# An attention loop on transposed scores, with maxima from a half-depth pass and float32 value products

## The chip, the cores and the metric

The kernel runs on one core of a Trainium2 chip, as one launch. The metric is the device time of that launch in microseconds. Five engines work side by side and wait for one another through semaphores: PE multiplies matrices, DVE and ACT do vector and scalar work and read PE's results out of PSUM, POOL does element-wise work on SBUF, and SP issues the DMAs here.

## The reference

The reference is a two-layer encoder trunk on 1024 tokens of width 1024, all in float32. Only the attention of the first layer is touched:

```python
def attend_block(q_blk):
    scores = jnp.einsum('bkgqd,bksd->bkgqs', q_blk, kt).astype(jnp.float32)
    p = jax.nn.softmax(scores, axis=-1).astype(vt.dtype)
    return jnp.einsum('bkgqs,bksd->bkgqd', p, vt)
...
return o @ w_o
```

There are 16 query heads and 4 key/value heads of 64 dimensions; q and k are normalised and rotated before. After the attention come the output projection, a cross-attention into 256 memory tokens and a gated MLP; the second layer has a pooling mixer in place of the attention.

## The kernel before

PE multiplies in a fast reduced form of float32 (`F32R`). To keep the precision, every operand x is split into a high part (rounded) and a low part (x minus high). `mm3` (lines 756 to 758) makes a product of three: high by high, high by low, low by high. Its helpers are `self.high` on ACT (line 669) and `self.low` on DVE (line 672). Most of the kernel's PE time is `mm3`.

The operands lie in slots: 20 tiles `R` of 128 x 2048, handed out whole or by halves by `Slots`. `self.scr()` gives scratch tiles of 128 x 1024, `self.psA()` PSUM tiles of two banks and `self.psB()` of one bank.

Stages are mostly ordered by `Plan`. A stage adds operations with a kind (which gives engine and assumed time), what they read, write and take; `Plan.run` then simulates the engines and writes the instructions of each engine in the order that comes out. On the chip the engines keep that order, whatever their real times are. The order within PE is the order in which the products were added.

The QKV stage (a `Plan`) makes q, k and v. For each token block k is split and transposed into `K[0]` and `K[1]`: 64 rows high on 64 rows low, and low on high. q is transposed into `Q[kv, half]` with high rows above low rows. So the two products `K[0]` and `K[1]` with q add up all four parts. v is kept as high and low columns in `V`. At the end of the stage three score units are computed ahead of the loop (`plan_scores`).

The attention loop is an order written out by hand (lines 1174 to 1296). A unit is 128 queries of one head. There are 128 units: four pairs of query blocks, 16 heads, two blocks. For each unit:

- `score` (line 789): four products of 512 columns put 128 queries x 1024 keys into a PSUM tile pA.
- `peak` (line 1189): DVE reduces to the negative maximum; `softmax`: ACT takes exp with the sum (line 1195), POOL the inverse (line 1197) and the scaling (line 1198).
- `turn` (line 1209): eight transposes on PE; ACT copies the high parts (line 1211) and DVE makes the low parts (line 1216) into `PT`.
- `values` (lines 1231, 1232), once for two units: 16 products of 256 columns, keys on the rows, high and low columns of v as weights; ACT and DVE add both halves (lines 1237, 1243), POOL splits the result into `OT` (lines 1246, 1247).

The loop is skewed: while PE computes the scores of a unit, the transposes and values are those of units two and three before it. Behind the loop `run` loads the output weights (`load_rows`) and starts the output products, two token blocks of each half first.

Of the kernel before, what the change touches and what calls it, by code (L numbers as in the profile page):

```python
# [16 lines left out]
P = 128  # L17
# [25 lines left out]
       *((h, g, t) for h in range(2) for g in range(4) if h or g > 1 for t in range(4 * h, 4 * h + 4)),  # L43
       ("V", 4), ("S", 0), ("V", 5), ("S", 1), ("V", 6), ("S", 2), ("V", 7))
LAG = 4
WARM = 20, 8
# [116 lines left out]
class Plan:  # L163
# [8 lines left out]
             "tiny": ("DVE", 0.1, 0.0, 0.1), "scale": ("POOL", 0.0, 0.45, 0.12), "load": ("SP", 0.0, 1.6, 2.3)}  # L172
# [458 lines left out]
class Kernel:  # L631
# [140 lines left out]
    def attention(self):  # L772
# [5 lines left out]
        units = [(j, hh, i) for j in range(NT // 2) for hh in range(NH) for i in range(2)]  # L778
        Q, prs, OT, sums = {}, {}, [], {}

        def score(u):
            j, hh, i = units[u]
            kv = hh // 4
            c0 = (j % 2 + 2 * i) * P
            q = R.v(Q[kv, j // 2], 4)[:, hh % 4, c0:c0 + P]
            s = self.psA()
            for kh in range(2):
                for part in range(2):
                    nc.tensor.matmul(s[:, kh * 512:(kh + 1) * 512], q,  # L789
                                     R.v(K[part][kh], 4)[:, kv],  # L790
                                     start=part == 0, stop=part == 1)
            return s

        with tc.tile_pool(name="qk", bufs=1, reuse_waits="tile") as qk, self.psum("psq", 1, 6) as self.ps:
# [222 lines left out]
            def plan_k(t, b):  # L1017
# [7 lines left out]
                def high():  # L1025
                    at[half] = R.get_half()
                    nc.scalar.activation(view(at[half])[:, :, 0:3:2], q3()[:, :, None, :].to_broadcast([P, 4, 2, HD]), AF.Copy)

                def low():
                    kst = view(at[half])  # L1030
                    nc.vector.tensor_tensor(out=kst[:, :, 1], in0=q3(), in1=kst[:, :, 0].bitcast(F32), op=OP.subtract)
# [5 lines left out]
            def plan_turn_k(t):  # L1037
                half = ("kst", t)
                for i in range(2):
                    b = ("kturned", t, i)  # L1040

                    def turn(i=i, b=b):
                        kst = R.hv(at[half])[:, :768].rearrange("p (h i c) -> p h i c", h=4, i=3)
                        p = at[b] = self.psB().rearrange("p (a b) -> p a b", a=4)
                        for h in range(4):
                            nc.tensor.transpose(p[:, h, :], kst[:, h, i:i + 2].rearrange("p a b -> p (a b)").bitcast(F32),
                                                self.ident)

                    def put(i=i, b=b):
                        o = R.v(K[i][t // 4], 4)[:, :, (t % 4) * P:(t % 4 + 1) * P]  # L1050
                        (nc.vector.tensor_copy if i else nc.scalar.copy)(o, at.pop(b))
# [3 lines left out]
            def plan_q(it, b):  # L1055
# [3 lines left out]

                def high():  # L1060
                    at[st] = qk.tile([P, 4, 2 * HD], F32R, name="qst", bufs=3)
                    self.high(at[st][:, :, :HD], q3())

                def low():
                    self.low(at[st][:, :, :HD], at[st][:, :, HD:], q3())
# [21 lines left out]
            def plan_scores(u):  # L1087
                j, hh, i = units[u]
                s, kv = ("s", u), hh // 4
                x = ("pr", u)  # L1090

                def emit():
                    at[s] = score(u)

                def biggest():
                    at["nm", u] = self.stat(1, "nm")
                    nc.vector.tensor_reduce(at["nm", u], at[s], axis=AX.X, op=OP.max, negate=True)

                def exp():
                    prs[u], at["sum", u] = self.scr(), self.stat(1, "sum")  # L1100
                    nc.scalar.activation(prs[u], at[s], AF.Exp, bias=at["nm", u], accum_out=at["sum", u])

                def inverse():
                    at["inv", u] = self.stat(1, "inv")
                    nc.vector.reciprocal(at["inv", u], at["sum", u])

                def scale():
                    nc.gpsimd.tensor_scalar(prs[u], prs[u], at["inv", u], 1.0, op0=OP.mult, op1=OP.mult)
                plan.add("product", 4, emit, [("KT", t, i) for t in range(NT) for i in range(2)] +
                         [("QT", kv, j // 2, t) for t in range(j // 2 * 4, j // 2 * 4 + 4)], [s], [("A", s)])  # L1110
                plan.add("tap", 1024, biggest, [s], [("nm", u)], uses=[s])
                plan.add("square", 1024, exp, [s, ("nm", u)], [x], [("scr", None)], [s], late=4.0)
                plan.add("tiny", 1, inverse, [x], [("inv", u)], late=6.0)
                plan.add("scale", 2.7, scale, [("inv", u), x], [x], late=7.0)

            def main():
# [7 lines left out]
                for it in QKV:  # L1124
                    kind, t = it[0], it[-1]
                    if kind == "S":
                        plan_scores(t)
# [44 lines left out]
            R.put(*sets[1])  # L1172

        self.ps = self.ctx.enter_context(self.psum("ps", 2, 4))
        with tc.tile_pool(name="at", bufs=1, reuse_waits="tile") as at:
            PT = [[at.tile([P, 2048], F32R, name=f"PT{i}{j}") for j in range(2)] for i in range(2)]
            def parts(u):
                return (x.rearrange("p (a b) -> p a b", a=8) for x in PT[u // 2 % 2])

            S, nm, T = {}, {}, {}  # L1180

            def scores(u):
                if u not in prs:
                    S[u] = score(u)

            def peak(u):
                if u in S:
                    nm[u] = self.stat(1, "nm")
                    nc.vector.tensor_reduce(nm[u], S[u], axis=AX.X, op=OP.max, negate=True)  # L1189

            def softmax(u):
                if u in S:
                    pr = prs[u] = self.scr()
                    rs = self.stat(1, "sum")
                    nc.scalar.activation(pr, S.pop(u), AF.Exp, bias=nm.pop(u), accum_out=rs)  # L1195
                    ri = self.stat(1, "inv")
                    nc.gpsimd.tensor_tensor(out=ri, in0=rs, in1=self.minus, op=OP.pow)
                    nc.gpsimd.tensor_scalar(pr, pr, ri, 1.0, op0=OP.mult, op1=OP.mult)  # L1198

            def pieces(u, g):  # L1200
                c = slice(u % 2 * P, (u % 2 + 1) * P)
                return (x[:, 4 * g:4 * g + 4, c] for x in parts(u))

            def turn(u, g):
                if u in prs:
                    p = T[u, g] = self.psB().rearrange("p (a b) -> p a b", a=4)
                    for k in range(4):
                        b = 4 * g + k
                        nc.tensor.transpose(p[:, k, :], prs[u][:, b * P:(b + 1) * P], self.ident)  # L1209
                    hi, _ = pieces(u, g)  # L1210
                    nc.scalar.copy(hi, p)  # L1211

            def low(u, g):
                if (u, g) in T:
                    hi, lo = pieces(u, g)
# [1060 lines left out]
```

## Time and profile before

| | us |
|---|---|
| median of 3 runs | 2498.35 (2497.17 to 2500.2) |
| span of the profiled execution | 2493.0 |
| median less that span | 5.35 |
| PE busy | 2474.6 |
| DVE busy | 1991.6 |
| ACT busy | 1351.0 |
| POOL busy | 462.1 |

The times of single instructions come from the profiled execution. The durations of matmuls overlap, since PE is a pipeline: the distance between the starts of two of them says what one costs. In rows on an instruction line, three durations with slashes are minimum, median and maximum in ns, followed by the first and the last start in us. In rows of groups the numbers behind the bar are busy us and mean ns, then idle time before them. In rows in order of time the first number is the start, the second the duration. A row of a stretch gives its length and then the busy time of PE, of the weight loads (PEld), DVE, ACT and POOL, the granted clock of PE (1.00 is full), and the DMA share.

### The profile page before, as it was taken

How to read it: one execution, taken by the hardware profiler on the slowest of the kernel's cores; microseconds unless marked ns; L12 is line 12 of the kernel's file. 1: busy time of each engine (PE TensorE's matmuls, PEld its weight loads, DVE VectorE, ACT ScalarE, POOL GpSimd, SP SyncE). 2: the span in 40 equal slices, each digit the busy share in tenths (PEclk: the TensorE clock that was granted, in tenths of full speed). 3: DMA queues.
4: the chain of work that ended last, by engine and by line, in shares of the span. 5: the costliest groups of instructions: out<-in, count | busy, mean ns of one | idle time of the engine just before them, and what ended most of it. 6: DMA issues, size and time to landing. Idle time of an engine off the chain costs nothing.

```text
span 2493.0 us, 37178 instructions
## 1 busy us (share of the span) xinstructions
PE 2474.6 (99%) x13510; PEld 2138.3 (86%) x13510; DVE 1991.6 (80%) x2839; ACT 1351.0 (54%) x2326; POOL 462.1 (19%) x658
## 2 busy tenths in 40 slices
PE   9999999999999999999999999999999999999998
PEld 9999999988899888888888888889888888888887
DVE  7879999974986389888889676997469888888875
ACT  6558888862655255455555334655345545554542
POOL 5767777731011000000000003102010000000001
PEclk9999999999999999999999999999999999999999
DMA  5300000042585124343258553388123324337852
GB/s 170 100 4 1 2 1 1 2 165 69 202 311 181 62 70 127 89 123 106 85 178 290 196 176 112 128 299 300 65 72 114 110 85 127 106 93 257 276 193 98
DMA packets 310124, 320.73 MB, mean 129 GB/s; under 512 B 13229, under 2 KB 244765, under 8 KB 309941
## 3 DMA queue, kind: packets, MB, share of 16 engines
q1 hardware_dynamic: 309941, 318.35, 38.8%
q8 instruction: 107, 1.75, 0.3%
q14 instruction: 76, 0.62, 0.1%
HBM read 230.91 MB, written 82.58 MB: 126 GB/s over the span
## 4 chain that ended last, share of the span: by engine, by line
PE 93%; issue 2%; DVE 2%; POOL 1%; ACT 1%; DMA 1%; SPq 0%; POOLq 0%; ACTq 0%; DVEq 0%
PE pB L756 22%; PE pB L758 22%; PE pB L757 22%; PE pA L789 5%; PE pB L1209 4%; PE pA L758 3%; PE pA L756 3%; PE pA L757 3%; PE pB L1231 2%; PE pB L1232 2%; PE pB L325 1%; DVE R L672 1%; PE pB L1072 1%; PE pA L2164 0%; DMA scr<-X 0%
## 5 line engine op out<-in xcount | busy, mean ns | idle before, releaser
L756 PE MATMUL pB<-R,R 128*128 128x512 f32 (+1 forms) x2732 | 1014.8, 371 | 1.8 <-ACT R L669 0.9
L758 PE MATMUL pB<-R,R 128*128 128x512 f32 (+1 forms) x2728 | 1007.6, 369 | 1.7 <-DVE R L672 1.6
L757 PE MATMUL pB<-R,R 128*128 128x512 f32 (+1 forms) x2732 | 1008.8, 369 | 0.2 <-DVE R L672 0.2
L756 PEld LDWEIGHTS pB<-R,R 128*128 128x128 f32 x2732 | 514.7, 188 | 90.9 <-ACT R L669 2.1
L758 PEld LDWEIGHTS pB<-R,R 128*128 128x128 f32 x2728 | 513.9, 188 | 89.5 <-DVE R L672 3.5
L757 PEld LDWEIGHTS pB<-R,R 128*128 128x128 f32 x2732 | 514.9, 188 | 87.1 <-DVE R L672 1.2
L669 ACT ACTIVATE R<-scr 128x512 fp32r<-128x512 f32 (+2 forms) x340 | 256.8, 782 | 214.9 <-DMA scr<-Gs 59.8
L729 POOL TENSOR_SCALAR ms<-ss 128x1 f32<-128x1 f32 (+2 forms) x97 | 32.1, 331 | 1651.7 <-ACT R L737 1279.9
L672 DVE TENSOR_TENSOR R<-X,R 128x512 fp32r<-128x512 f32 x374 | 252.0, 685 | 67.8 <-ACT R L669 67.1
L669 ACT ACTIVATE R<-X 128x512 fp32r<-128x512 f32 x374 | 231.8, 630 | 132.9 <-PE pB L757 64.0
L672 DVE TENSOR_TENSOR R<-scr,R 128x512 fp32r<-128x512 f32 (+2 forms) x328 | 275.0, 867 | 26.6 <-ACT R L669 26.2
L439 ACT COPY scr<-pB 128x512 f32<-128x512 f32 x156 | 91.3, 585 | 180.6 <-PE pB L758 173.3
L1852 DVE TENSOR_TENSOR X<-pB,X 128x512 f32<-128x512 f32 (+1 forms) x145 | 99.2, 685 | 80.4 <-PE pB L758 79.6
L1216 DVE TENSOR_TENSOR PT<-pB,PT 128x512 fp32r<-128x512 f32 x256 | 159.1, 683 | 4.2 <-ACT PT L1211 2.9
L1189 DVE TENSOR_REDUCE nm<-pA 128x1 f32<-128x1024 f32 x125 | 152.2, 1218 | 4.3
L756 PE MATMUL pA<-R,R 128*128 128x512 f32 (+1 forms) x420 | 150.6, 359 | 0.0
L758 PE MATMUL pA<-R,R 128*128 128x512 f32 (+1 forms) x420 | 150.2, 358 | 0.0
L757 PE MATMUL pA<-R,R 128*128 128x512 f32 (+1 forms) x420 | 149.9, 357 | 0.0
L1195 ACT ACTIVATE scr<-pA,nm 128x1024 f32<-128x1024 f32 x125 | 142.4, 1139 | 5.6 <-DVE nm L1189 3.5
L789 PE MATMUL pA<-R,R 128*128 128x512 f32 x512 | 144.7, 404 | 0.3 <-ACT scr L1195 0.3
L1198 POOL TENSOR_SCALAR scr<-scr,inv 128x1024 f32<-128x1024 f32 x125 | 141.2, 1129 | 12.3
L1211 ACT CAST PT<-pB 128x512 fp32r<-128x512 f32 x256 | 131.0, 600 | 1.2 <-PE pB L1209 1.2
(184 smaller groups left out, 3582.5 us busy)
## 6 DMA issues: line engine op xcount, KB each, us to landing
X<-in_ffn_w_up SPq DMA_DIRECT2D x82, 512.0 KB
Gs<-X SPq DMA_DIRECT2D x105, 256.0 KB
scr<-in_ffn_w_down SPq DMA_DIRECT2D x45, 512.0 KB
scr<-Gs SPq DMA_DIRECT2D x35, 512.0 KB
scr<-in_xattn_w_kv SPq DMA_DIRECT2D x32, 512.0 KB
scr<-Gs SPq DMA_DIRECT2D x42, 384.0 KB
scr<-in_attn_w_qkv SPq DMA_DIRECT2D x22, 512.0 KB
Wt<-scr SPq DMA_DIRECT2D x44, 256.0 KB
```

Of the source, the lines that this page charges most:

```text
L669: self.nc.scalar.activation(hi, src, AF.Copy)
L672: self.nc.vector.tensor_tensor(out=lo, in0=src, in1=hi.bitcast(F32), op=OP.subtract)
L756: mm(out, ah, bh, start=start, stop=False)
L757: mm(out, ah, bl, start=False, stop=False)
L758: mm(out, al, bh, start=False, stop=stop)
L789: nc.tensor.matmul(s[:, kh * 512:(kh + 1) * 512], q, R.v(K[part][kh], 4)[:, kv], start=part == 0, stop=part == 1)
L1189: nc.vector.tensor_reduce(nm[u], S[u], axis=AX.X, op=OP.max, negate=True)
L1195: nc.scalar.activation(pr, S.pop(u), AF.Exp, bias=nm.pop(u), accum_out=rs)
L1198: nc.gpsimd.tensor_scalar(pr, pr, ri, 1.0, op0=OP.mult, op1=OP.mult)
L1209: nc.tensor.transpose(p[:, k, :], prs[u][:, b * P:(b + 1) * P], self.ident)
L1211: nc.scalar.copy(hi, p)
L1216: nc.vector.tensor_tensor(out=lo, in0=T.pop((u, g)), in1=hi.bitcast(F32), op=OP.subtract)
```

## The change

The loop is rebuilt as a `Plan` on scores that have keys on the rows and queries on the columns, so that no transposes are needed behind the softmax. A group is 512 queries (`half`) and two heads; there are 16 groups, 8 of each half.

- **K and Q.** `K[0]` now holds the high part twice, on both row halves. `K[1]` holds the low part on 64 rows and, written by POOL (`plan_ones`), a row of ones below. In `Q` the high rows stand above for one head of a pair and below for the other.
- **Maxima.** `peaks` (line 789 in the new file) computes high by high only, for the two heads at once: one on rows 0 to 63, the other on rows 64 to 127, each a product of 64 rows and 512 columns into its own bank. DVE reduces (`biggest`), the two key halves are joined (`joined`), and `shift` brings them as a row to slot half `qm` by eight DMAs of 128 elements, next to two DMAs that copy the high rows of q there. Those of group 0 are made in the QKV stage, where the three score units stood, those of later groups five steps ahead.
- **Scores.** `plan_scores` makes 128 keys x 512 queries with two products: `K[0]` with Q, and 65 rows of `K[1]` with `qm`. The row of ones adds the negative maximum, so ACT takes exp without a bias and writes float32 to `pt`.
- **Values.** v's two parts are added once into `V32` (POOL). `plan_values` multiplies in full float32, `V32` as weights of 64 columns; the two heads go to the two column halves (output rows 0 to 63 and 64 to 127). DVE and POOL add up the exps of the eight key blocks (`acc`), and `plan_sum` sums them over the keys with a float32 product against ones.
- **Scaling.** The sums go by DMA to 8 x 128, DVE takes the inverse, and by a DRAM tile they come back spread over 64 rows each (`spread`, `inverse`, `park`, `back`). POOL multiplies, ACT and DVE split into `OT`.
- **Output weights.** The first half of them is loaded and split inside the loop, during the last group but one (`plan_rows`).

The core of the diff:

```diff
-       ("V", 4), ("S", 0), ("V", 5), ("S", 1), ("V", 6), ("S", 2), ("V", 7))
+         for it in ([q, ("S", n // 3)] if n % 3 == 2 else [q])),
+       ("V", 4), ("V", 5), ("V", 6), ("V", 7))
...
+        def peaks(G, n, S):
+            half, m = GROUPS[G]
+            q, t, kh = R.v(Q[m // 2, half], 4), n // 2, n % 2
+            for x in range(2):
+                rows = slice(x * HD, (x + 1) * HD)
+                nc.tensor.matmul(S[:, x * 512:(x + 1) * 512], q[rows, m % 2 * 2 + x, t * P:(t + 1) * P],
+                                 R.v(K[0][kh], 4)[rows, m // 2], start=True, stop=True)
...
+        def shift(G, h):
+            half, m = GROUPS[G]
+            q, qm = R.v(Q[m // 2, half], 4), R.hv(h).bitcast(F32)
+            for x in range(2):
+                nc.sync.dma_start(out=qm[:HD, x * 512:(x + 1) * 512],
+                                  in_=q[x * HD:(x + 1) * HD, m % 2 * 2 + x].bitcast(F32))
+            nm = NM.pop(G)
+            for i in range(8):
+                nc.sync.dma_start(out=qm[HD:HD + 1, i * P:(i + 1) * P], in_=nm[:, i:i + 1].bitcast(F32))
...
-                            nc.tensor.transpose(p[:, h, :], kst[:, h, i:i + 2].rearrange("p a b -> p (a b)").bitcast(F32),
-                                                self.ident)
+                            src = kst[:, h, 2] if i else kst[:, h, :2].rearrange("p a b -> p (a b)")
+                            nc.tensor.transpose(p[:HD if i else P, h, :], src.bitcast(F32), self.ident)
...
+                    nc.tensor.matmul(T[b], R.v(K[0][kt // 4], 4)[:, m // 2, cols], R.v(Q[m // 2, half], 4)[:, m % 2 * 2 + x],
+                                     start=True, stop=False)
+                    nc.tensor.matmul(T[b], R.v(K[1][kt // 4], 4)[:HD + 1, m // 2, cols],
+                                     R.hv(ring[G % 4])[:HD + 1, x * 512:(x + 1) * 512], start=False, stop=True)
...
+                    for kt in ks:
+                        for x in range(2):
+                            nc.tensor.matmul(O[G][x * HD:(x + 1) * HD], V32[:, kt, m // 2], E[G, kt][:, x * 512:(x + 1) * 512],
+                                             start=kt == 0, stop=kt == NT - 1)
...
+                for n, (G, d) in enumerate(steps):
+                    plan_scores(G, 0, 2 * d)
+                    plan_scores(G, 1, 2 * d)
+                    ahead = [((n + 5) // 4, (n + 5) % 4 * 2 + i) for i in range(2)]
+                    if ahead[0][0] <= last:
+                        plan_peaks(*ahead[0])
+                    plan_scores(G, 0, 2 * d + 1)
+                    if ahead[0][0] <= last:
+                        plan_peaks(*ahead[1])
+                    plan_scores(G, 1, 2 * d + 1)
+                    if n:
+                        plan_values(*steps[n - 1])
+                    if G and d == 2:
+                        plan_sum(G - 1)
+                    if G == last - 1:
+                        plan_rows(d // 2, d % 2)
```

The old loop (`parts`, `scores`, `peak`, `softmax`, `pieces`, `turn`, `low`, `values`, `add` and their order by hand) is removed.

More of the change, by code (lines that the diff above doesn't have):

```diff
@@ L1084, in plan_q, with plan_peaks @@
                 return plan_turn
[L1087 to L1090, printed above, removed]
+            def plan_peaks(n):
+                b = ("s", n)
                 def emit():
[L1093 to L1114, printed above, removed]
@@ new lines, in emit @@
+                    at[b] = self.psA()
+                    peaks(0, n, at[b])
+                plan.add("product", 1, emit, [("KT", t, 0) for t in range(n % 2 * 4, n % 2 * 4 + 4)] + [("QT", 0, 0, n // 2)],
+                         [b], [("A", b)])
+                plan.add("tap", 1024, lambda: biggest(0, n, at.pop(b)), [b], [("nm", n)], uses=[b])
+                if n < 7:
+                    return
+                plan.add("tiny", 1, lambda: joined(0), [("nm", i) for i in range(8)], ["nm"])
@@ L1126, in main @@
                     if kind == "S":
[L1127 removed]
+                        plan_peaks(t)
+                        if t < 2:
+                            plan_ones(t)
                         continue
```

302 lines of the change are left out of this document (171 added, 131 removed).

## The prediction

> **What bounds the kernel now.** I read the busy shares first, then the busy time by stretch, then the chain of work that ended last, then the instructions of the attention loop one by one.
>
> ```profile
> PE 2474.6 (99%) x13510; PEld 2138.3 (86%) x13510; DVE 1991.6 (80%) x2839; ACT 1351.0 (54%) x2326; POOL 462.1 (19%) x658
> 230.00:500.00 270.00, 270.00 (x1975) 250.29 (x1974) 258.44 (x346) 227.68 (x443) 191.98 (x247) 1.00 0.00 1
> 187.75 1.75 PE pB L1209 x16
> ...
> 505.20 1.75 PE pB L1209 x16
> L1209 PE MATMUL pB<-ident,scr x1024: 270/273/328, 178.5 to 525.0; 128*128 128x128 f32 x171
> L1232 PE MATMUL pB<-PT,R x512: 274/278/384, 184.9 to 528.1; 128*128 128x256 f32 x171
> ```
>
> PE is busy 99% of the span, and all 270 of 270 us in the middle of the attention loop, at full clock (1.00). DVE has 258 of 270 there. The loop runs from the first transpose at 178.5 to the last value product at 528.1: 350 us. Two units (a unit is one head and 128 queries) recur every (505.20 - 187.75) / 58 = 5.47 us.
>
> ```profile
> 299.84 0.28 PE L1232 MATMUL pB<-PT,R 128*128 128x256 f32 x1
> ...
> 301.48 0.28 PE L1232 MATMUL pB<-PT,R 128*128 128x256 f32 x1
> 834.30 0.39 PE L758 MATMUL pB<-R,R 128*128 128x512 f32 x1
> 834.62 0.32 PEld L1664 LDWEIGHTS pB<-ident,scr 44*128 44x128 f32 x4 [0.35 <-issue]
> 834.62 0.44 PE L1664 MATMUL pB<-ident,scr 44*128 44x44 f32 x4
> 835.00 0.50 PE L756 MATMUL pB<-R,R 128*128 128x512 f32 x1
> 835.10 0.19 PEld L757 LDWEIGHTS pB<-R,R 128*128 128x128 f32 x1
> ...
> 835.33 0.39 PE L757 MATMUL pB<-R,R 128*128 128x512 f32 x1
> ...
> 836.46 0.39 PE L756 MATMUL pB<-R,R 128*128 128x512 f32 x1
> ```
>
> What counts is the distance between starts, since the durations overlap. A product of 512 columns takes (836.46 - 835.33) / 5 = 0.226 us, one of 256 columns (301.48 - 299.84) / 14 = 0.117, a transpose 1.75 / 16 = 0.109. Two units need 8 x 0.226 + 16 x 0.109 + 16 x 0.117 = 5.43 us of the 5.47: the stage is PE's instruction list, and what the change does to that list decides.
>
> **The change part by part.** A step of the new loop handles one group (512 queries, two heads) and two key blocks; there are 16 groups of 4 steps. By the built order PE does, in each: score, score, peaks, score, peaks, score, values. A score is two 512-column products, peaks are two products on the two row halves, values four float32 products on the two column halves, and once a group two more of these give the sums.
>
> *Products alone.* Scores: 512 x 0.226 = 115.7 us. Peaks: if the halves run together, 15 groups x 8 pairs x 0.226 = 27.1. For a float32 product of 512 columns the nearest rows are the mixer's:
>
> ```profile
> 1554.08 1.94 PE L2164 MATMUL pA<-scr 128*128 128x112 f32 x16
> ...
> 1565.11 1.95 PE L2164 MATMUL pA<-scr 24*128 24x16 f32 x16
> ```
>
> Eight products leave 16 records there, two for each, and with 112 or with 16 columns these stand 0.11 us apart ((1.94 - 0.275) / 15): there the weight load governs. A record therefore streams its 112 columns in at most 0.11, so 512 in at most 0.51; at least it takes 0.226. The product is bounded by 0.45 and 1.01. I take two passes for each record, the largest whole number that fits: 0.904. With halves together, 128 pairs of values and 18 of sums cost 146 x 0.904 = 132.0. Sum 274.8 us, 75 less than 350.
>
> *Changing the array's division.* The same rows show what that leaves out. L1664 is a product on 44 rows between products on 128. The streaming of L758 ends at 834.30 + 0.226 = 834.53; L756 streams from 835.33 - 0.226 = 835.10. Of these 0.57 us the four transposes take 4 x 0.06 (their loads: (0.32 - 0.14) / 3). There and back costs 0.33 us: the load of a new form isn't begun beneath the old one. A second place, with one transpose on 8 rows:
>
> ```profile
> 1449.38 0.39 PE L758 MATMUL pA<-R,R 128*128 128x512 f32 x1
> ...
> 1449.70 0.22 PE L2068 MATMUL pB<-ident,scr 8*128 8x8 f32 x1
> ...
> 1450.20 0.40 PE L757 MATMUL pA<-R,R 128*128 128x512 f32 x1
> ...
> 1450.44 0.40 PE L758 MATMUL pA<-R,R 128*128 128x512 f32 x1
> ```
>
> From 1449.61 to 1450.20 - 0.24 = 1449.96 are 0.35, less 0.06: 0.29. I take 0.31 for a round trip, on row halves as on column halves; no row shows column halves, so there it lies between 0 and 0.33. On top the first weights are exposed: 0.10 (835.00 to 835.10), half of that for 64 columns. And halves may start one after the other: the second load of peaks adds 0 to 0.10, and since the two records of one float32 product share their half, four products fill four or five places of 0.452. So peaks 0.31 + 0.10 + 0.226 + 0.05 = 0.69 (0.64 to 0.74), values 0.31 + 0.05 + 2.04 = 2.40 (2.17 to 2.62).
>
> The Trainium skill (TensorEngine Tiling (Array Packing), Key Properties) says that changing the tiling mode, not just the tile, drains TensorE. By that rule the column halves pay as well; rows agree for row halves, and no run here shows the other. Without it the values would be 0.36 cheaper, 23 us over the 64 steps.
>
> A step is 8 x 0.226 + 2 x 0.69 + 2.40 + 0.23 (a quarter of the sums) = 5.82 us, a group 23.3. Two units of before, times four, were 21.9.
>
> *The wait that is added.* The second product of a group's first score reads qm, which gets the group's negative maxima by ten DMAs inside SBUF from SP's queue. PE works in order, so all of the group stands behind it. The last peaks of a group are emitted in the third step of the group before. Behind them come two reductions and the joining minimum on DVE, eight 512-byte DMAs, and their landing.
>
> ```profile
> L1189 DVE TENSOR_REDUCE nm<-pA 128x1 f32<-128x1024 f32 x125 | 152.2, 1218 | 4.3
> L1720 DVE TENSOR_TENSOR X<-X,scr 128x1024 f32<-128x1024 f32 x22 | 26.8, 1219 | 0.1
> L343 POOL TENSOR_TENSOR X<-X,X 128x512 f32<-128x512 f32 x6 | 7.8, 1293 | 31.2 <-DVE X L343 31.2
> L1458 ACT ACTIVATE X<-pA,nm 128x256 f32<-128x256 f32 x64 | 29.5, 478 | 26.7 <-DVE nm L1453 26.7
> L1195 ACT ACTIVATE scr<-pA,nm 128x1024 f32<-128x1024 f32 x125 | 142.4, 1139 | 5.6 <-DVE nm L1189 3.5
> L2140 SPq DMA_DIRECT2D scr<-X x18: 668/777/1396, 1508.8 to 1547.9; - x18
> 1509.80 0.68 SPq L2142 DMA_DIRECT2D scr<-X  x1
> 1513.99 1.06 ACT L737 ACTIVATE R<-scr 128x1024 fp32r<-128x1024 f32 x1 [1.21 <-DMA scr<-X]
> ```
>
> DMAs from SBUF to SBUF hold SP 0.67 to 0.78 us, even the small one of L2142 (8 rows), which landed some 3.5 us after its issue ended. From the third step's start the second peaks end after 2.8, both reductions (1.22 each) after 4.2, the minimum after 4.4; then 8 x 0.68 = 5.4 of issue, and 3 to 3.5 of landing. With two full steps ahead (2 x 5.59), a group can't be shorter than 11.2 + 4.4 + 5.4 + 3.2 = 24.2 us. That exceeds PE's 23.3, so a group loses about 0.7: I take 24.0. SP's other five DMAs of a group stand behind these eight and have a whole group's time.
>
> The loop: 15 x 24.0 + 20 for the last group (no peaks, three pairs of sums) + 1.4 for two early peaks = 381, less 350: +31.
>
> *Other engines.* DVE per group: 8 reductions and 4 adds at 1.22, splits and a reciprocal of some 2: 16.6. ACT: 16 exps of 512 columns, 0.70 each between the rows of 256 and 1024, and copies: 13. POOL: three adds of 1024 at about 2.5 (twice L343's row), one product of 512 at 1.29: 9. All lie beneath 23 us of PE and cost nothing while PE is that slow; beneath 17 us DVE would be close.
>
> ```profile
> L1007 POOL TENSOR_TENSOR qn<-qn,rb x40: 724/736/1721, 22.7 to 170.9; 128x256 f32<-128x256 f32 x40
> ```
>
> POOL's and DVE's instructions on two SBUF operands can hold one another up (1721 beside a median of 736). If each of DVE's four adds waited 2.5, DVE would need 26 a group, so its cover is the thinnest; I take no wait, because POOL's adds start behind DVE's and end before the next.
>
> *Outside the loop.* In the QKV stage three score units (12 x 0.226 = 2.7) make way for 8 peaks alone (5.5): +2.8. The low halves of K are transposed on 64 columns, 8 blocks with a round trip: +2.5. The output weights' four loads move ahead in SP's queue, in front of the shift of the last group; their splits fall to ACT and DVE, which have room, and the stall they save is 0.7. The last group's sums, four DMA hops and the scaling take some 15 us, covered by the first four output products (24 x 0.226 = 5.4 each), which need the other half of the queries. I allow +1 for both ends. Together +6.
>
> The profiled execution: 2493.0 + 31 + 6 = 2530. The median shown, 2498.35, lies 5.35 above that span: 2535. I forecast 2532, a little below, since the landing of 512-byte pieces is probably shorter.
>
> **The rivals.**
>
> *Faster: the switches vanish in this stream.* If the weights of the halves load beneath other products, a step is 1.81 + 0.45 + 1.81 + 0.23 = 4.30. The DMA chain then decides: 2 x 4.07 + 4.0 + 5.4 + 3.2 = 20.7 a group, loop 15 x 20.7 + 17 = 328, -22: 2476. With a short chain a group is 17.2 and the time 2428. For it: L1664 and L2068 are small transposes, two places in the whole trace. Against: both show the same. With no staggering and a hidden chain the sign turns at a round trip of 0.27; with the chain, near zero. The Trainium skill (TensorE: Matmul & The Clock Gate, Part 3) has packed products start 4 ns apart, which is this case; no run here shows it.
>
> *The halves don't run together.* Peaks are then 0.86, values 3.98, sums 0.45 a step: 8.0, a group 31.9, the loop 508 and the time 2662. Nothing in the trace shows two products at once.
>
> *The chain is longer.*
>
> ```profile
> 1519.71 6.42 DMA scr<-X
> ```
>
> This landing took 6.4 us, and L2140's worst issue is 1.40. At 1.0 each (between median and worst) and 6.4 of landing a group is 11.2 + 4.4 + 8.0 + 6.4 = 30.0: the loop 471, the time 2624. For it: pieces of four bytes from 128 partitions, which no row shows. Against: that row is four transfers of many rows.
>
> *The float32 products cost half* (0.45): values 1.4, step 4.7, with the chain 22.2 a group; loop 350, time 2504.
>
> **How the numbers follow.** Forecast 0.53, covering 2500 to 2560; no switches 0.25; halves not together 0.08; longer chain 0.09; cheap float32 0.05. The range 2455 to 2585 leaves out the end of the first rival with a short chain, the second, and half of the third: 0.2. Slower by over 0.2% (5 us, about what three runs from 2497 to 2500 can tell): 0.70; faster 0.25; same 0.05 (the edges of the first and the last rival).
>
> **What would show it.** Right: PE gaps of about 0.3 us at each change between scores, peaks and values, a step of 5.5 to 6 us, and one stall a group of a microsecond or two at the first score, ended by a DMA into the maxima's row. Wrong: peaks 0.23 us apart from the scores around them; values in 3.6 us or more; stalls ended by DVE or POOL.

## The result and the profile after

| | before | after |
|---|---|---|
| median, us | 2498.49 (2497.17 to 2500.2, 4 runs) | 2520.93 (2519.0 to 2523.07, 4 runs) |
| profiled span, us | 2493.0 | 2518.7 |

The ratio is 1.0089, with a 95% interval of 1.0075 to 1.0103: slower by 22 us. The forecast was 2532, slower, so sign and size were near. The terms of the sum were not: the loop costs less than forecast, what lies around it more.

The busy shares after, then three stretches (up to the loop, the loop, behind it), first of before and then of after. The columns are length, then busy us and instructions of PE, weight loads, DVE, ACT and POOL, then PE's granted clock.

```profile
PE 2485.2 (99%) x12302; PEld 1962.5 (78%) x12302; DVE 1936.9 (77%) x2645; ACT 1229.3 (49%) x2070; POOL 355.6 (14%) x407
```

```profile
0.00:178.50 178.50, 174.20 (x1450) 171.73 (x1450) 143.88 (x330) 101.89 (x213) 116.43 (x156) 1.00 0.29 96
178.50:528.20 349.70, 348.94 (x2549) 322.64 (x2549) 332.52 (x446) 294.83 (x573) 243.12 (x312) 1.00 0.03 10
528.20:2493.00 1964.80, 1951.49 (x9515) 1643.91 (x9513) 1515.19 (x2065) 954.32 (x1542) 102.59 (x190) 1.00 0.47 153
```

```profile
0.00:183.90 183.90, 177.67 (x1453) 172.78 (x1453) 149.33 (x335) 99.65 (x208) 113.61 (x156) 0.99 0.31 96
183.90:543.90 360.00, 352.90 (x1336) 142.96 (x1336) 274.85 (x247) 176.22 (x320) 137.22 (x62) 0.98 0.12 28
543.90:2518.70 1974.80, 1954.60 (x9515) 1646.73 (x9513) 1512.76 (x2064) 953.39 (x1543) 104.81 (x190) 1.00 0.47 153
```

The 25.7 us of span are 5.4 in the QKV stage, 10.3 in the loop and 10.0 behind it. ACT, DVE and POOL have much less to do in the loop (ACT 176 us instead of 295), and PE has half the instructions; it is busy 352.90 of 360.00 all the same.

One steady step of the loop on PE, in order of time:

```profile
305.62 0.50 PE L1222 MATMUL pT<-R,R 128*128 128x512 f32 x1
305.96 0.40 PE L1224 MATMUL pT<-R,R 65*128 65x512 f32 x1
306.19 0.40 PE L1222 MATMUL pT<-R,R 128*128 128x512 f32 x1
306.42 0.39 PE L1224 MATMUL pT<-R,R 65*128 65x512 f32 x1
306.74 0.51 PE L789 MATMUL pA<-R,R 64*128 64x512 f32 x2
307.18 0.50 PE L1222 MATMUL pT<-R,R 128*128 128x512 f32 x1
307.52 0.40 PE L1224 MATMUL pT<-R,R 65*128 65x512 f32 x1
307.85 0.49 PE L789 MATMUL pA<-R,R 64*128 64x512 f32 x2
308.27 0.50 PE L1222 MATMUL pT<-R,R 128*128 128x512 f32 x1
308.61 0.40 PE L1224 MATMUL pT<-R,R 65*128 65x512 f32 x1
308.94 1.94 PE L1260 MATMUL pO<-pt,V 128*64 128x512 f32 x8
310.81 0.50 PE L1222 MATMUL pT<-R,R 128*128 128x512 f32 x1
```

A step takes 310.81 - 305.62 = 5.19 us. Score products stand 0.235 apart where nothing lies between them. By the array's form I mean whether products use all its rows and columns, halves of its rows (the maxima) or halves of its columns (the values). Across the maxima the two neighbours stand 307.18 - 306.42 = 0.76 apart, and the first of them behind a change is followed after 0.34 instead of 0.235: 0.76 + 0.34 - 2 x 0.235 = 0.63 for a pair of maxima. Both its records start together (x2 in 0.51 us where one alone lasts about 0.50). The values cost, in the same way, 310.81 - 308.61 + 0.34 - 2 x 0.235 = 2.07, with eight records that start in four places of (1.94 - 0.592) / 3 = 0.449 (0.592 is what the last record lasts). Of 5.19 us, 8 x 0.235 + 2 x 0.226 + 4 x 0.452 = 4.14 are streaming; 1.05 go to six changes of the array's form, with the weight loads that a change leaves uncovered.

The chain that ends at a group's first score (all engines, the lines that belong to it):

```profile
270.01 2.34 DVE L795 TENSOR_REDUCE nm<-pA 128x2 f32<-128x1024 f32 x2
272.39 0.17 DVE L802 TENSOR_TENSOR nmr<-nm 128x8 fp32r<-128x8 f32 x1
272.59 5.03 SPq L814 DMA_DIRECT2D R<-nmr  x8
279.27 0.47 PE L1224 MATMUL pT<-R,R 65*128 65x512 f32 x1 [0.29 <-DMA R<-nmr]
```

The two reductions start late because DVE is at other work until 270.01. The eight small DMAs hold SP 5.03 us and the last lands 279.27 - 277.62 = 1.65 later, a little behind PE. Values of the same place in a group stand 22.0 apart (303.75 and 325.77): four steps of 5.19, 0.87 for the sums, and some 0.4 for this wait.

The start of the loop, waits and then stretches:

```profile
186.59 0.47 PE L1224 MATMUL pT<-R,R 65*128 65x512 f32 x1 [1.52 <-DMA R<-nmr]
189.16 0.76 PE L1224 MATMUL pT<-R,R 65*128 65x512 f32 x1 [1.87 <-DMA R<-nmr]
```

```profile
183.00:190.00 7.00, 3.12 (x14) 1.38 (x12) 2.85 (x4) 1.60 (x4) 4.67 (x2) 0.94 0.09 2
190.00:196.00 6.00, 6.00 (x14) 3.03 (x14) 2.45 (x2) 2.94 (x5) 0.00 (x0) 0.50 0.01 3
196.00:203.00 7.00, 7.00 (x17) 2.37 (x16) 3.58 (x3) 1.21 (x3) 0.00 (x0) 0.52 0.00 0
```

PE waits twice for group 0's row copies, and then works for 13 us at half clock. The first values start at 199.06, where two early pairs and two steps' scores (183.9 + 0.7 + 2 x 3.12) would have brought them at 190.8; the second follow 6.95 later instead of 5.19. Together some 10 us.

The end of the loop (SP, DVE, PE and a stretch):

```profile
553.80 4.55 SPq L2324 DMA_DIRECT2D X<-in_x  x8
558.65 0.76 DVE L675 TENSOR_TENSOR R<-scr,R 128x256 fp32r<-128x256 f32 x2 [3.19 <-ACT R L672]
561.45 1.29 DVE L1733 TENSOR_TENSOR X<-pB,X 128x512 f32<-128x512 f32 x2 [1.44 <-DMA X<-in_x]
572.08 1.97 PE L328 MATMUL pB<-ident,X 128*128 128x128 f32 x8 [6.09 <-DVE X L323]
560.00:575.00 15.00, 8.91 (x39) 7.31 (x38) 3.38 (x6) 3.45 (x7) 1.50 (x4) 0.77 0.65 244
```

The products end at 543.9 and the next four output products cover 21.7 us. Their first sum with X comes only at 561.45: the loads of X stand in SP's queue behind the last group's small DMAs, and DVE stands behind that group's split. PE then waits 6.09 us for the normalised rows and loses more at a clock of 0.77.

### The profile page after: what moved, and what is told of

It is laid out like the page before. It is cut to its first block, busy times and chain, and to the rows that moved or that the text cites. A ratio compares the mean times of both kernels' runs of the same rounds, so it can differ in the third digit from the quotient of the medians.

```text
span 2518.7 us, 33712 instructions
## 1 busy us (share of the span) xinstructions
PE 2485.2 (99%) x12302; PEld 1962.5 (78%) x12302; DVE 1936.9 (77%) x2645; ACT 1229.3 (49%) x2070; POOL 355.6 (14%) x407
## 4 chain that ended last, share of the span: by engine, by line
PE 82%; DVE 8%; issue 3%; DMA 3%; SPq 2%; POOL 0%; ACT 0%; POOLq 0%; DVEq 0%; ACTq 0%
PE pB L759 22%; PE pB L761 22%; PE pB L760 22%; PE pA L761 3%; PE pA L759 3%; PE pA L760 3%; DVE nm L795 2%; SPq L814 2%; DVE R L675 2%; DVE scr L1267 2%; PE pO L1260 1%; PE pT L1222 1%; PE pB L328 1%; PE pT L1224 1%; PE pA L789 1%
## 5 line engine op out<-in xcount | busy, mean ns | idle before, releaser
L672 ACT ACTIVATE R<-scr 128x512 fp32r<-128x512 f32 (+3 forms) x376 | 272.9, 753 | 235.8 <-DMA scr<-Gs 59.3
L675 DVE TENSOR_TENSOR R<-scr,R 128x512 fp32r<-128x512 f32 (+3 forms) x364 | 321.4, 911 | 29.7 <-ACT R L672 29.1
L1232 ACT ACTIVATE pt<-pT 128x512 f32<-128x512 f32 x256 | 148.8, 599 | 151.3 <-PE pT L1224 149.6
L795 DVE TENSOR_REDUCE nm<-pA 128x2 f32<-128x1024 f32 x128 | 150.6, 1211 | 27.7 <-PE pA L789 27.6
L1270 POOL TENSOR_TENSOR scr<-scr 128x1024 f32<-128x1024 f32 x46 | 115.2, 2504 | 191.9 <-DVE scr L1267 191.9
L1260 PE MATMUL pO<-pt,V 128*64 128x512 f32 x512 | 127.1, 619 | 0.0
L1222 PE MATMUL pT<-R,R 128*128 128x512 f32 x256 | 121.9, 476 | 0.0
L1222 PEld LDWEIGHTS pT<-R,R 128*128 128x128 f32 x256 | 48.7, 190 | 85.9 <-issue 53.5
```

The source lines that it names most:

```text
L672: self.nc.scalar.activation(hi, src, AF.Copy)
L675: self.nc.vector.tensor_tensor(out=lo, in0=src, in1=hi.bitcast(F32), op=OP.subtract)
L795: nc.vector.tensor_reduce(NM[G][:, 2 * n:2 * n + 2], S.rearrange("p (x k) -> p x k", x=2), axis=AX.X, op=OP.max, negate=True)
L1222: nc.tensor.matmul(T[b], R.v(K[0][kt // 4], 4)[:, m // 2, cols], R.v(Q[m // 2, half], 4)[:, m % 2 * 2 + x], start=True, stop=False)
L1232: nc.scalar.activation(E[G, kt][:, x * 512:(x + 1) * 512], T.pop(b), AF.Exp)
L1260: nc.tensor.matmul(O[G][x * HD:(x + 1) * HD], V32[:, kt, m // 2], E[G, kt][:, x * 512:(x + 1) * 512], start=kt == 0, stop=kt == NT - 1)
```

## The experiments

Theory: the array's changes of form set the step, the chain of maxima and row copies sets the group, and waits at both ends of the loop cost the rest. A run's expectation names its own theories A, B and C. Rivals stand with each run.

**Maxima joined** (changes of form three instead of six a step). PE's order in a step, in short:

```diff
-   score, score, peaks, score, peaks, score, values(n - 1)
+   peaks, peaks, score, score, score, score, values(n - 1)
```

> One thing is moved: both pairs of maxima products of a step now stand together, right behind the values of the step before, with the four scores behind them. The same products run; the array changes its form three times in a step instead of six. Theory A (each change of form costs time of its own): in the changed kernel a pair of maxima takes .64 us out of the score stream, of which .23 is streaming, and the values take 2.07 for 1.71 of streaming. Joined, values and four maxima products should take 1.71 + 2 x .23 + .36, and up to .2 for the change from column halves to row halves: 2.5 to 2.7. The step goes from 5.19 to 4.4 to 4.6 us, the loop from 360 to 310 to 325, the time from 2521 to 2471 to 2486; if the chain of reduce, join and row copies (about 10.2 us from the last maxima to the first score that needs them, against 10.3 that then lie between) becomes late, up to 2496. Theory B (form changes are free, the products alone and their waits for banks make the .64): the step stays at 5.19, the time within 5 us of 2521.

Measured: 2494.22 us (ratio to before 0.9983, 0.9974 to 0.9993). PE in order of time:

```profile
309.79 1.94 PE L1260 MATMUL pO<-pt,V 128*64 128x512 f32 x8
311.66 0.73 PE L789 MATMUL pA<-R,R 64*128 64x512 f32 x4
312.32 0.50 PE L1222 MATMUL pT<-R,R 128*128 128x512 f32 x1
...
314.40 1.94 PE L1260 MATMUL pO<-pt,V 128*64 128x512 f32 x8
```

The same products in 4.61 us: 0.47 over streaming for three changes, against 1.05 for six, 0.16 to 0.18 each on the mean. The maxima follow the values after 1.87, 0.06 more than their streaming, so the changes aren't equally dear. The step is what theory A says (4.4 to 4.6). The time isn't in its 2471 to 2486, and the reason that it allowed for up to 2496, late row copies, is not the one: waits for them of over 0.2 us are two, 0.43 at the loop's start and 0.69 at 489.04. The largest wait stands near the end, with half clock for 6.83 us from 496.48 on:

```profile
499.61 0.79 PE L1222 MATMUL pT<-R,R 128*128 128x512 f32 x1 [5.69 <-ACT pt L1232]
```

Without this wait and what the half clock costs the time would be some 2494 - 5.7 - 3.4 = 2485, an estimate from these rows. The rest is small: the step with the sums takes 6.0, since the maxima behind them wait for a PSUM tile ("0.26 <-ACT scr L1297"), and single steps wait for DVE's reduction (5.59 at 294.46).

**Joined, six steps ahead.** As above with

```diff
-   ahead = [((n + 5) // 4, (n + 5) % 4 * 2 + i) for i in range(2)]
+   ahead = [((n + 6) // 4, (n + 6) % 4 * 2 + i) for i in range(2)]
```

> As the kernel with the joined maxima, and the maxima run six steps ahead of the scores instead of five. Theory A (array form alone sets the step once the chain has room): steps of 4.4 to 4.6 us with no longer first step in a group, 5 to 15 us below the joined kernel's time if that had stalls, the same time if it had none: 2465 to 2485. Theory B (form changes free): the step stays 5.19 and only the first-step stalls go, some .4 us x 15 = 6: 2515. Theory C (the row copies, ten of about .6 us in one queue for each group, bound the group by themselves): group time stays above 20 us however early the maxima are.

Measured: 2491.24 us (0.9971, 0.996 to 0.9981). No wait for the row copies is left and a group takes 19.95 (252.57 to 272.52), so theory C is out. The time is 6 us above theory A's range: near the end, as in the run before, ACT waits for a scratch tile that POOL's add holds, and the exps behind it are late. ACT, then PE:

```profile
495.87 0.59 ACT L1279 COPY scr<-pO 128x512 f32<-128x512 f32 x1 [4.65 <-POOL scr L1270]
497.01 0.80 PE L1222 MATMUL pT<-R,R 128*128 128x512 f32 x1 [2.98 <-ACT pt L1232]
498.16 3.68 PE L1260 MATMUL pO<-pt,V 128*64 128x512 f32 x8
```

After such a wait the values take 3.68 us, half clock, instead of 1.94.

**Maxima over all rows** (high and low part of q with the high part of k; no change of form for them).

```diff
-   matmul(S[..], q[rows, ..], K[0][rows, ..])
+   matmul(S[..], q[:, ..], K[0][:, ..])
```

> The maxima are taken over all 128 rows by two plain products instead of one pair on the row halves; nothing is moved. The array keeps one form through scores and maxima. Theory A (form change costs): an insertion of maxima takes 2 x .235 = .47 instead of .64; 120 insertions in the loop give -20 us: 2501 (2495 to 2507). Theory B (form changes cost nothing and the halves' concurrency is what pays): .24 more for each insertion, +28 us: 2549.

Measured: 2515.58 us (1.0064, 1.0046 to 1.0081). The step falls to 4.85 as theory A says, but the time by 5 us, not 20. From the third group on PE waits for the row copies in every group, 0.85 to 1.23 us:

```profile
316.27 0.50 PE L1223 MATMUL pT<-R,R 65*128 65x512 f32 x1 [0.85 <-DMA R<-nmr]
```

A group takes 22.16 (252.57 to 274.73), as long as in the changed kernel. There PE's own 21.6 and the chain were equal within 0.4 us; what PE saves here became a wait.

**All rows, six steps ahead.** Both edits together.

> As the kernel with maxima over all 128 rows (2515.6 us), with the maxima six steps ahead of the scores instead of five. There a step took 4.85 us, so four and the sums (.86) make 20.3, but a group took 22.1 (252.57 to 274.73), with PE waiting about 1 us for the row copies at two places of each group. Theory A (the chain of reduce, join, row copies and landing ends last, and the saving of .34 a step went into it): with a step more of room a group takes 20.3, 14 groups x 1.8 = -25: 2490 (2486 to 2496). Theory B (DVE, POOL or ACT holds a group at some 22 us): 2515.

Measured: 2483.4 us (0.9935, 0.9919 to 0.9952): 32 less than without the step more of room, and below the expected range. PE, then the stretch at the loop's start:

```profile
267.98 1.94 PE L1259 MATMUL pO<-pt,V 128*64 128x512 f32 x8
...
288.25 1.94 PE L1259 MATMUL pO<-pt,V 128*64 128x512 f32 x8
```

```profile
183.00:203.00 20.00, 18.07 (x74) 10.76 (x75) 17.14 (x16) 9.12 (x16) 6.43 (x3) 1.00 0.12 14
```

A group takes 20.27, PE's own sum: theory A. Beyond the expected 25 us the start gives 2.2: the two more pairs of early maxima fill it, one wait of 0.67 for the row copies is left, the clock stays at 1.00, and the first values come at 192.6 (194.8 in the run before). The last group gives some 4 more: its row copies were waited for there (1.41 and 0.95 us, with half clock behind), and no longer are.

**Values by head.**

```diff
-   for kt in ks:
-       for x in range(2):
+   for x in range(2):
+       for kt in ks:
```

> The four values products of a step are issued head 0, head 0, head 1, head 1 instead of alternating; the same products. Theory A (a float32 product of 512 columns costs about .85 us and only neighbours on different column halves run together): two of the four run together instead of two pairs, 1.71 becomes 2.55, +.85 x 64 = +54 us: 2575; if none run together 3.4, +108: 2629. Theory B (each float32 product simply costs .43 here, one after the other): no change, 2521.

Measured: 2521.89 us in one run, no change, with eight records in 1.94 us as before. Theory A's form of "neighbours only" falls. Theory B is not shown by it, since the halves could run together whatever the order. The next run decides.

**One half.**

```diff
+   y = x if kt == 0 else 0
-   matmul(O[G][x * HD:(x + 1) * HD], V32[..], E[G, kt][.., x])
+   matmul(O[G][y * HD:(y + 1) * HD], V32[..], E[G, kt][.., x])
```

> Of the two heads' values only the first product of head 1 goes to column half 1; all its other products are added into column half 0, so that from the second step of a group on all four products of a step stand on the same half (head 0's output holds both heads' values, head 1's nearly none). Same number of products and passes. Theory A (a float32 product takes .90 us and two on different halves run together, in whatever order they are issued): in three steps of four the four products take 3.6 us instead of 1.8, +1.8 x 48 = +87: 2608. Theory B (a float32 product takes .45 us, each by itself, and the pairs of records that start together are the two passes of one product): no change, 2521.

The two heads' outputs are then mixed, so the run serves for the time alone.

Measured: 2606.69 us in one run, 86 more, where theory A said 87. Two neighbouring steps in order of time, all products on one half and then the first step of a group:

```profile
329.75 3.65 PE L1261 MATMUL pO<-pt,V 128*64 128x512 f32 x8
...
336.64 2.79 PE L1261 MATMUL pO<-pt,V 128*64 128x512 f32 x8
```

On one half the records start (3.65 - 0.592) / 7 = 0.44 apart. A group takes 27.6 instead of 22.0, which is 3 x 1.71 for the steps on one half and 0.85 for its first step, less the wait for the row copies; theory A had 3 x 1.8 alone, so that the total fits so well is partly luck. The mechanism stands: a float32 product of 512 columns does cost two records of 0.44 to 0.45, and the two halves run together, whichever head comes first in the queue.

**Group 0's maxima early.**

```diff
-   S entries behind Q products 2, 5, 8, 11, 14, 17, 20, 23
+   S entries behind Q products 2, 5, 8, 11, 14, 16, 18, 20; the join behind 23
```

> Group 0's maxima are taken a few products earlier in the QKV stage (the last pair and its reduction before the last three Q products instead of behind them); the join and the row copies still stand behind the last Q weights, whose place they take. In the changed kernel DVE did the last reduction at 180.33, the row copies were issued from 182.22, PE waited 1.52 and 1.87 us for them, and the clock in 185 to 204 was .64. Theory A (these two waits also bring the clock down): waits and slow clock go, -9: 2512 (2510 to 2515). Theory B (the clock falls there for another reason): -3: 2518. Theory C (the place in the weights' buffer gates the copies, not the reduction): 2521.

Measured: 2519.3 us in one run. The edit didn't reach what it was to test: DVE's order still has the last reduction at 179.89 and the copies are issued at 181.78, 0.44 earlier, no more than the whole stage is (the loop's first product starts at 183.07 instead of 183.91), with the same two waits (1.92, 1.88) and the same half clock. What became of the start is told by the kernel six steps ahead.

**The last group's DMAs from GpSimd's queue.**

```diff
+   queue = nc.sync if G < last else nc.gpsimd
-   nc.sync.dma_start(..)      # spread, park, back
+   queue.dma_start(..)
```

> The last group's small DMAs (spread, park, back: five) are issued from GpSimd's queue, so the loads of X are no longer behind them in SyncE's. In the changed kernel the X loads were issued at 553.80 behind the last of these, the first sum with X followed at 561.45, and at 572.08 PE had been idle for 6.09 us waiting for the normalised rows, clock .77 in 560 to 575. Theory A (that queue is the cause): X loads at about 546, 6 of idle and 2 to 3 of slow clock go: 2512 (2510 to 2516). Theory B (the X loads wait for memory that the loop's tiles held, or the stall is set by the sums and the row copies behind them): within 3 us of 2521.

Measured: 2520.52 us in one run: nothing. The loads of X did go 6.4 us earlier, but by that queue the hops took longer (scaling at 563.98), and DVE stood behind the last split:

```profile
547.37 4.93 SPq L2325 DMA_DIRECT2D X<-in_x  x8
565.74 0.76 DVE L675 TENSOR_TENSOR R<-scr,R 128x256 fp32r<-128x256 f32 x2 [9.46 <-ACT R L672]
571.25 1.97 PE L328 MATMUL pB<-ident,X 128*128 128x128 f32 x8 [5.64 <-DVE X L323]
```

**The last group inverted where it stands.** In short:

```diff
+   if G == last:
+       nc.vector.reciprocal(ON[G][:, 512:], ON[G][:, 512:])
+   else: spread, inverse, park, back
```

> Only the last group's sums are inverted where they stand (512 columns on 128 rows by one instruction of VectorE) instead of being spread to 8 rows, inverted, parked and fetched back by five small DMAs; the other groups are as in the changed kernel. By the reciprocal's row (.93 us for 128 columns) it takes about 3.7 us on DVE, and five issues, three landings and a wait behind the weights' splits go; the last group's splits should end about 551 to 553 instead of 558.65, with the X loads no longer behind those DMAs in SyncE's queue. Theory A (both the X loads and ACT's and DVE's wait for the last group's scaling hold up the first sums; with the loads alone moved, ACT and DVE were held up 12.8 and 9.5 us by the scaling and nothing was gained): first sum with X at about 553, the idle time of 6.1 us at 572 and the slow clock behind it go: 2512 (2509 to 2515). Theory B (the stall comes from the normalisation's own chain after the sums): 2521.

Measured: 2515.85 us (1.0071, 1.0054 to 1.0088), 5 less where theory A said 9, and just outside its range. The inverse took 3.35 us, the first sum came at 553.99, and the wait for the normalised rows fell from 6.09 to under 0.3. In its place the second half of the output weights was late, now behind six loads of X:

```profile
558.87 0.50 PE L759 MATMUL pB<-R,R 128*128 128x512 f32 x1 [1.89 <-ACT R L680]
560.13 0.79 PE L760 MATMUL pB<-R,R 128*128 128x512 f32 x1 [0.76 <-DVE R L681]
```

**All rows, six ahead, last group direct.** The three edits together.

> Maxima over all rows, six steps ahead (2483.4), and the last group's sums inverted where they stand. That kernel has the same stall behind the loop (6.6 us of PE waiting for the normalised rows). Theory A: -8 against it: 2475 (2472 to 2479). Theory B (the stall is the normalisation's own): 2483.

Measured: 2478.79 us (0.9925, 0.991 to 0.9939), 4.6 less than without the last edit, where 8 was expected. The stall that it was to mend is 5.87 us there, not 6.6, and here it is gone, with the same new wait for the weights (2.45 and 0.76).

**The second weights in front.** The same with

```diff
-   if t == NT - 2:      # in run: where the second half of the weights is asked for
+   if t == 2:
```

> Maxima over all rows, six steps ahead, the last group inverted where it stands (2478.8), and the second half of the output weights asked for behind two loads of X instead of six. In that kernel PE now waits 2.45 and .76 us at 524.2 and 525.4 for the split of these weights, with a clock of .83 in 520 to 530. Theory A (the place in SyncE's queue holds them): both waits and the slow clock go, 3.2 + 1.7 = 5: 2474 (2472 to 2477). Theory B (their landing behind two loads of X takes as long, or the normalised rows become late in their place): 2478.

Measured: 2477.07 us (0.9913, 0.9897 to 0.993), 1.7 less than without the edit, where theory A said 5: a hair outside its range and next to theory B's 2478. By the trace both waits for the weights and their half clock are gone, so the place in the queue was their cause; what theory B had in their place is one wait of 0.61 us, at full clock:

```profile
529.28 1.09 PE L328 MATMUL pB<-ident,X 128*128 128x128 f32 x8 [0.61 <-DVE X L323]
```

Part of the gain is lost again in the second layer (below). This version beats both kernels, the one before by 21 us.

**Output weights behind the loop.** `plan_rows` left out, the load behind the loop as before.

> The changed kernel without the early loads of the output weights during the last group but one; they are loaded behind the loop as before. In the changed kernel SyncE's queue waited 8.8 us at such a load for a scratch buffer that GpSimd held, with the last group's row copies behind it; PE waited 1.01 and .49 us at 520.9 and 522.1 and the next values took 3.48 us instead of 1.9. Theory A (the load in front of the row copies is the cause): these 3.3 us go, the last group's first step takes 5.2 to 5.6 instead of 7.5, and up to 5 us come back behind the loop where the weights are late: 2517 to 2523. Theory B (the chain of maxima is late there anyway): the first step stays at 7.5 and the time rises by what the late weights cost.

Measured: 2525.01 us in one run, 4 more, which alone would be near what runs of one kernel differ by. The last group still waits for its row copies, 1.42 us, and the late weights cost waits of up to 2.96 in three places:

```profile
520.02 0.47 PE L1224 MATMUL pT<-R,R 65*128 65x512 f32 x1 [1.42 <-DMA R<-nmr]
567.52 0.50 PE L759 MATMUL pB<-R,R 128*128 128x512 f32 x1 [2.96 <-ACT R L680]
```

Theory B: the chain is late there anyway, as the step in front of that group has no maxima left and is shorter (4.80). The early load holds up little; that it is worth more rests on these waits and on one run.

## Why the prediction was right, and where not

- **Changes of form: right.** A pair of maxima was put at 0.69 (0.64 to 0.74) and takes 0.63. Column halves pay too: the values' streaming is 1.81, their place in the stream 2.07, so 0.26 goes to the change there and back, within 0 to 0.33. The run over all rows shows the change for the row halves by itself; for the column halves it is read from these distances alone. This agrees with the Trainium skill (TensorEngine Tiling (Array Packing), Key Properties), by which a change of the tiling mode drains TensorE; it gives no price. The rival without changes (2476; with the +6 for what lies outside the loop, which its sum leaves out, 2482) is what the joined kernel moves towards: three changes fewer in a step bring a net 27 us.
- **Values: too dear.** 2.40 was put, 2.07 measured: four places of 0.452 instead of four or five, and 0.26 instead of 0.36 for the change and the exposed weights. The pass count (0.904 for a product) and the halves running together were right, as the run on one half shows; so the rivals "halves don't run together" and "cheap float32" are out.
- **The step:** 5.59 without the sums was forecast, 5.19 measured; PE's group 23.3 against 21.6.
- **The chain: right mechanism, wrong size.** The eight issues took 5.03 instead of 5.4 and the landing 1.65 instead of 3.2. These two alone would make 22.3 of the 24.2, but two more terms were off and cancel. From the third step's start at 266.77 to the end of the joined minimum at 272.56 are 5.8 instead of 4.4, for the reductions stand behind an add and two low parts on DVE, which the prediction gave no wait. And from the product that waits (279.27) to the third step of its own group (288.92) are 9.65 instead of 11.2, as the steps are shorter and it is the second product that waits. So 9.65 + 5.8 + 5.05 + 1.65 = 22.15, and a group took 22.0 instead of 24.0. The sign named for it, one stall a group at the first score, is there, but 0.3 to 0.5 us long instead of one or two. PE and the chain end together, as forecast, and the edit to all rows showed it: 0.34 saved in each step, nothing saved in a group.
- **The loop: +31 forecast, +10 measured.** Fifteen groups took 334.8 (184.57 to 519.38) instead of 360, though some 10 of that went at the start, which the forecast didn't have. The last group took 24.6 instead of 20: it waits 1.01 and 0.49 us for its row copies and then takes 3.55 us for the values at 523.42 that take 1.94 elsewhere.
- **QKV stage: +5.3 forecast, +5.4 measured, partly by luck.** The two terms were not told apart. The stage's first projection product starts at 9.68 instead of 8.10, after a wait for ACT of 2.22 us instead of 0.87, and the clock is at half from 11.6 to 15.0, where it is full before; neither is in the sum. With the same QKV code the first score comes at 183.25 in the run with the last group direct and at 184.57 here.
- **Behind the loop: the failed step.** "I allow +1 for both ends" and "covered by the first four output products" were wrong. The last group's hops are covered as far as PE's products are concerned; but the loads of X, the weights' splits and DVE's first sums stood behind them in their engines' queues, and the normalisation behind those. Up to the second layer's mixer these waits are nearly all of it, by the same product in the changed kernel and in the one with the second weights in front:

```profile
1577.65 1.94 PE L2254 MATMUL pA<-scr 128*128 128x112 f32 x16
1532.65 1.94 PE L2259 MATMUL pA<-scr 128*128 128x112 f32 x16
```

From the loop's end (528.20, 543.93 and 506.60) it is 1554.08 - 528.20 = 1025.9 in the kernel before, 1033.7 in the changed one and 1026.0 with the waits mended: 7.8 lost, 7.7 brought back. The other 2.2 us come later. There the clock is at half for 3.4 us from 1591.97 in the changed kernel (0.76 in 1590 to 1597) and for 6.8 us in the mended one (0.77 in 1540 to 1555), and full in the kernel before. Why it falls there stays open: the run with all rows six steps ahead keeps 1.00 in that place.

So a loop 21 us too long and ends 9 us too short came to 11 us of span (2518.7 against 2530). The changes of form and the chain are real, and they ate up what the shorter list of products saved. But they didn't make the kernel slower: a steady group takes 22.0 where the same work took 21.9 before, and without the 10 us at the start and the 3 in the last group the loop would have been 347, against 349.7. What makes the kernel slower is 10 at the loop's start, 3 in the last group, 10 behind the loop and 5.4 in the QKV stage, less these 2.7. Of this the forecast had 5.3 for QKV and 1 for the ends. So the size came from errors that cancelled, and the sign, too, was in good part luck.

## What to carry to other kernels

Count how often the array changes its form, not only the products: the same products in an order with half the changes were a net 27 us faster here. When a saving on the bounding engine moves nothing, look for a chain of equal length beside it and give that chain room first; all rows alone brought 5 us, with one more step of lead 38. And at the end of a stage ask of every in-order queue what stands behind the last slow step, for the next stage's first loads and sums do.

## What the runs showed of the hardware that was not expected

- The two column halves ran together even when both products of one half were issued ahead of both of the other: eight records in four places (1.94 us) in either order. On one half records stand 0.44 apart, so in strict order the second half could not begin before the first half's last record, and eight would need seven places. The Trainium skill (TensorE: Matmul & The Clock Gate, Part 3) calls matmuls strictly first in, first out; these rows speak against it between halves, if PE's queue has the order of the kernel, for the trace doesn't name a record's half. That packed products start practically together, which the same part says, agrees (x2 in 0.51 us).
- Waits of PE of 1.5 and 1.9 us within 4 us were followed by 13 us at half clock (0.50 and 0.52), although PE was busy through them; one of 2.98 was followed by values that took 3.68 instead of 1.94. So a wait at a stage's edge can cost two or three times its length. It needn't be one long wait: in the joined kernel six steps ahead waits of 0.63 to 1.09 us, one behind the other, were followed by half clock at 189.2, with PE busy 1.50 of the 3.4 us before. Waits of up to 1.23 us, one in each group of 22 us, left the clock at 1.00 (all rows, 192 to 516). Not every fall has such waits in front of it: the one at 1591.97 has one of 0.55.
- A DMA of 512 bytes within SBUF held SP's queue 0.63 us and landed 1.65 us after the last issue; by GpSimd's queue, in one run, the last group's split came some 7 us later (565.74 against 558.65).
